# Four turns per head in the first mixer's recurrence, with the next head's decays spread over them

## The chip, the core and the metric

One core of one Trainium2 chip. The metric is the device time of one execution in microseconds; lower is better. The engines are TensorE (PE), VectorE (DVE), ScalarE (ACT), GpSimd (POOL) and SyncE (SP), which here issues the loads.

## What is computed

Two transformer blocks in a row on 256 tokens of width 1024. The first has a mixer (a gated linear recurrence in both directions and a latent attention, merged by gates), a mixture of 64 experts and a gated side input; the second a convolution and window attention. The change lies in the first mixer, whose core is, cut to what matters:

```
z = rmsnorm(x, ln_mix) @ w_in
q_a, f_fw, f_bw, i_a, og_a, c_q, c_kv, k_rope, gate_a, gate_b = split(z)
# recurrence, 4 heads of 128, each direction, chunks of 64
g = cumsum(log_f)
decay = exp(where(lower, g[t] - g[s], -inf))
scores = einsum('tk,sk,tsk->ts', q, k, decay)        # k = 1 - f
o = (q * exp(g)) @ state + scores @ v
o_hg = rmsnorm(o_fw + o_bw, hg_onorm) * silu(og_a)
y_a = o_hg @ w_oA
# latent attention, 8 heads of 96
qm = rope(rmsnorm(rmsnorm(c_q) @ w_uq));  km = rope(rmsnorm([rmsnorm(c_kv) @ w_ukv, k_rope]))
y_b = attention(qm, km, vm) @ w_oB
x = x + (sigmoid(gate_a) * y_a + sigmoid(gate_b) * y_b) @ w_out
```

## The kernel before

All matmuls of the big projections are exact to float32 by splitting: `split` (L185) casts a weight slice of 128x512 to `hi` on ACT (L188) and computes the rest `lo` on DVE or, by the pattern in `sub_turn`, on POOL (L192); "v" means all on DVE, "vg" turn about. `gemm_t` (L235, matmuls L247 to L249) and `gemm_nat` (L197, L209 to L211) take eight such slices for one 512-wide chunk and yield after each two. I call two slices, 24 matmuls in `gemm_t`, a step. Weights come in tiles of 1 MB through a ring of buffers (`wload`, L108); a tile's load is issued when the buffer's last reader is done.

The order on PE is that of the program text (`manual_schedule`, L347). `weave` (L263) runs generators turn about, so the yields decide how matmuls of several parts are mixed. On the other engines a planner orders the instructions by its own estimate of when each is ready, and may run one ahead of its place in the text; `tc.issue_after(ins)` puts the instructions of a block behind `ins` on that engine, and only on that.

The stages around the change, in order:

1. `first_lane` (two decay chunks of `w_in`, 8 steps, then logarithms L589 and scans L594) woven with `latent_prepare` (L432): norms of the latent vectors, projection of keys, then of queries, and `head_norm` (L403) for each half of the tokens. `head_norm` squares on ACT, sums and scales on DVE, makes four rotary products on POOL (L425 to L428) and combines them on DVE (L429, L430).
2. `modulation(16, 8)` (matmuls L655), then two steps of `second_lane` (the q chunk), then the rest of `second_lane` (q, v, og) woven with `latent_attend` (L496), which also takes the pieces of head 0's decays. In `second_lane` the two halves of k are added (L633), multiplied by q, and summed by 128x1 matmuls with `ones` (L640) into a PSUM bank.
3. `recurrence` (L764) woven with `modulation(0, 16)` and `gate_lane` (four gate chunks and `w_oB`, 20 steps): in each round one turn of the recurrence, one modulation step while there are any, one gate step.

`decayed(h)` (L679) makes a head's factors: R and L for seven levels by subtraction (R on DVE L692, L on POOL L694), exponentials on ACT (L698, L700, L704 to L716), R times q on DVE (L717), L times k per level (L721, levels 0, 2, 4 on POOL, the others on DVE), and the cross factors CR and CL (L724, L726). In `recurrence` a head has three turns: the diagonal, the cross scores (L802) and levels 0 to 3 (L812), each level copied into `sct` under a mask by DVE (L815); levels 4 to 6; then `attend` for the head before (L768), `finish` for the one before that (L787), and all of the next head's decays at once.

PSUM has four banks "mm", three "ps", one "ob".

Of the kernel before, what the change touches and what calls it, by code (L numbers as in the profile page):

```python
# [20 lines left out]
P = 128  # L21
# [58 lines left out]
def kernel(ctx: ExitStack, tc: tile.TileContext, a: dict, out: bass.AP, dbg=None):  # L80
# [182 lines left out]
    def weave(*lanes):  # L263
        live = list(lanes)
        stop = object()
        while live:
            for lane in list(live):
                g, n = lane
                for _ in range(n):
                    if next(g, stop) is stop:  # L270
                        live.remove(lane)
                        break

    def both(done):
        def each(ps):
            for i in range(NT):
                done(i, ps[i])
        return each
# [124 lines left out]
    def head_norm(dst, which, i):  # L403
# [23 lines left out]
        G.tensor_tensor(t[:, 2], x2, cb, op=ALU.mult)  # L427
        G.tensor_tensor(t[:, 3], x1, sb, op=ALU.mult)  # L428
        V.tensor_tensor(x1, t[:, 0], t[:, 1], op=ALU.subtract)  # L429
        V.tensor_tensor(x2, t[:, 2], t[:, 3], op=ALU.add)  # L430

    def latent_prepare():  # L432
# [26 lines left out]
        V.tensor_copy(kgain[:, 64:96], rrow("k_norm")[:, 64:96])  # L459
        yield  # L460
        khl = [split(sp, wuk, c * 512, 512) for c in range(2)]
        for i in range(NT):
# [10 lines left out]
            V.tensor_copy(kn[:, i * MH:(i + 1) * MH, 64:96], misc[:, i, 384:416][:, None, :].to_broadcast([P, MH, 32]))  # L473
            head_norm(kn, 1, i)
        yield
        for c in range(2):
            qhl = [split(sp, wuq, k * 768 + c * 384, 384) for k in range(2)]
            for i in range(NT):
                o = bank("ps")
                for k in range(2):  # L480
# [6 lines left out]
                               o[:, :384].rearrange("p (h d) -> p h d", h=4))  # L487
        for i in range(NT):
            head_norm(qn, 0, i)
        dump("qm", qn)  # L490
# [100 lines left out]
    def scan_decays(d):  # L591
# [5 lines left out]
        if d:  # L597
            V.tensor_scalar(ge[:, 1, :, 0:4], last, -1.0, None, op0=ALU.mult)
            V.tensor_add(ge[:, :, :, 4], ge[:, :, :, 0], ge[:, :, :, 1])
            V.memset(gxv[:, :, :, 0:1], 0.0)  # L600
        else:
            V.tensor_copy(ge[:, 0, :, 0:4], last)

# [19 lines left out]
    def first_lane():  # L623
        yield from gemm_t(sp, hT, chunk("w_in", 0), take_decay(0))
        yield from gemm_t(sp, hT, chunk("w_in", 1), take_decay(1))
        log_decays()
        for d in range(2):
            scan_decays(d)

    def second_lane():  # L630
        yield from gemm_t(sp, hT, chunk("w_in", 2), take_q)
        qk = qg[:, 1]
        V.tensor_tensor(qk, kT[:, 0], kT[:, 1], op=ALU.add)  # L633
        V.tensor_tensor(qk, qk, qT, op=ALU.mult)
        yield from gemm_nat(sp, hT, chunk("w_in", 3), 512, take_v)
        b = bank("ps")
        for h in range(HGH):
# [41 lines left out]
    def decayed(h):  # L679
# [38 lines left out]
        for l in range(NLEV):  # L718
            eng = V if l % 2 or l == 6 else G
            Ls = both_sides(L[:, l], l)  # L720
            eng.tensor_tensor(Ls, Ls, sides(kT, (X, HGH * 256 + X + (1 << l)), 1, l), op=ALU.mult)  # L721
            if l in (0, 3):
                yield
# [3 lines left out]
        yield R, L, CR, CL  # L727

    def decayed_at_once(h):
        return list(decayed(h))[-1]  # L730

# [8 lines left out]
    cc = cc_cm.__enter__()  # L740
    sub_turn[1] = "vg"
    weave((modulation(16, 8), 1))
    second = second_lane()
    weave((some(second, 2), 1))
    weave((latent_attend(), 1), (second, 1))

# [17 lines left out]
    def recurrence():  # L764
# [29 lines left out]
        for h in range(HGH):  # L794
# [9 lines left out]
            nc.scalar.copy(cr, dg[:, :256])  # L804
            scores[h] = (sct, cr)
            for l0 in range(0, NLEV, 2):
                n = min(2, NLEV - l0)
# [6 lines left out]
                for l in range(n):  # L814
                    V.copy_predicated(sct, msk[:, l0 + l][:, None, :].to_broadcast([P, NT, P]),  # L815
                                      b[:, l * 256:(l + 1) * 256].rearrange("p (i t) -> p i t", i=NT))
                if l0 in (2, 6):
                    yield
            if h >= 1:
                attend(h - 1)  # L820
            if h >= 2:
                finish(h - 2)
            if h + 1 < HGH:
                RL[h + 1] = decayed_at_once(h + 1)
            yield
# [1047 lines left out]
```

## Time and profile before

| | us |
|---|---|
| median of 3 runs (lowest, highest) | 1122.52 (1121.57, 1122.76) |
| the profiled execution, own time | 1120.88 |
| its span, first to last instruction | 1119.1 |
| PE busy in the span | 1026.4 (92%) |
| DVE busy | 570.7 (51%) |
| ACT busy | 423.3 (38%) |
| POOL busy | 294.9 (26%) |
| stages: first mixer to about 262 us, experts to about 745 us, then side input and second block | |

Times are microseconds from the start of the span. An engine's busy time covers pipelined matmuls, whose ends are modelled: a matmul of 0.28 us can start 0.12 us after the one before. The granted clock is a share of TensorE's 2.4 GHz. In a timeline a row joins like instructions in sequence; brackets give the idle time of the engine before it and what ended that.

### The profile page before, as it was taken

What the parts mean: (1) busy time and instruction counts of PE and PEld (TensorE: products, weight loads), DVE (VectorE), ACT (ScalarE), POOL (GpSimd) and SP (SyncE); (2) the same over time, 40 slices, a digit from 0 to 9 for tenths busy, and PEclk for the clock granted to TensorE, in tenths of its full rate; (3) what the DMA queues carried; (4) which work ended last, traced back from release to release, by engine and by line L of the source; (5) the groups of instructions that cost most, each with busy time, mean ns of one, the idle gap of its engine ahead of it and who ended that gap; (6) DMA issues with size and microseconds to landing.
All of it is one profiled execution on the core that took longest, in us unless ns stands there. A gap on an engine that the chain in (4) does not pass through costs nothing.

```text
span 1119.1 us, 17631 instructions
## 1 busy us (share of the span) xinstructions
PE 1026.4 (92%) x6844; PEld 730.9 (65%) x6848; DVE 570.7 (51%) x1157; ACT 423.3 (38%) x875; POOL 294.9 (26%) x255
## 2 busy tenths in 40 slices
PE   8999989998999768999987788799999999999997
PEld 6887679985444224444333233267889989999996
DVE  6977996364333212221122232285847798852465
ACT  6767854440101031010110020263457546545553
POOL 1554474440000000000000000003543363554462
PEclk9999999999999889999997899998999999999999
DMA  9673566878999999999999999963554343345531
GB/s 351 236 264 114 220 233 263 339 293 330 421 421 419 421 420 421 420 422 420 421 420 419 421 421 418 421 268 99 171 201 167 136 139 131 128 160 184 184 114 39
DMA packets 47259, 321.49 MB, mean 287 GB/s; under 512 B 5761, under 2 KB 6273, under 8 KB 9410
## 3 DMA queue, kind: packets, MB, share of 16 engines
q1 hardware_dynamic: 47090, 320.04, 72.5%
q8 instruction: 56, 0.92, 0.4%
q14 instruction: 33, 0.27, 0.1%
q0 software_dynamic: 80, 0.26, 0.1%
HBM read 319.23 MB, written 1.05 MB: 286 GB/s over the span
## 4 chain that ended last, share of the span: by engine, by line
PE 58%; DMA 23%; DVE 12%; ACT 3%; issue 3%; POOL 1%; SPq 0%; DVEq 0%; POOLq 0%; ACTq 0%
DMA w<-in_w_dram 21%; PE mm L249 8%; PE mm L247 8%; PE mm L248 8%; PE mm L1257 5%; PE mm L209 3%; PE mm L210 3%; PE mm L211 3%; PE ps L1224 3%; PE mm L1297 3%; PE ps L1240 2%; PE mm L971 2%; DVE lo L192 2%; PE ps L174 2%; DMA w<-in_w_ple_proj_dram 2%
## 5 line engine op out<-in xcount | busy, mean ns | idle before, releaser
L188 ACT CAST hi<-w 128x512 fp32r<-128x512 f32 (+2 forms) x340 | 205.3, 616 | 177.8 <-PE mm L248 127.4
L192 POOL TENSOR_TENSOR lo<-w,hi 128x512 fp32r<-128x512 f32 x144 | 200.4, 1394 | 237.9 <-ACT hi L188 231.5
L192 DVE TENSOR_TENSOR lo<-w,hi 128x512 fp32r<-128x512 f32 (+2 forms) x196 | 148.4, 767 | 113.5 <-ACT hi L188 103.7
L1257 PE MATMUL mm<-w,xe 128*32 128x512 f32 x1024 | 128.7, 641 | 29.3 <-DMA w<-in_w_dram 21.9
L247 PE MATMUL mm<-h,hi 128*128 128x256 f32 x448 | 129.5, 289 | 0.0
L249 PE MATMUL mm<-h,lo 128*128 128x256 f32 x448 | 126.7, 283 | 0.1
L248 PE MATMUL mm<-h,hi 128*128 128x256 f32 x448 | 126.6, 283 | 0.0
L1257 PEld LDWEIGHTS mm<-w,xe 128*32 128x32 f32 x1024 | 30.5, 114 | 114.9 <-issue 61.7
L1279 DVE SCALAR_TENSOR_TENSOR th<-th,mm 128x256 f32<-128x256 f32 x16 | 6.7, 421 | 179.6 <-ACT th L1278 179.6
L247 PEld LDWEIGHTS mm<-h,hi 128*128 128x128 f32 x448 | 85.6, 191 | 3.1 <-issue 3.1
L249 PEld LDWEIGHTS mm<-h,lo 128*128 128x128 f32 x448 | 85.6, 191 | 0.3 <-DVE lo L192 0.3
L248 PEld LDWEIGHTS mm<-h,hi 128*128 128x128 f32 x448 | 85.7, 191 | 0.0
L1278 ACT ACTIVATE th<-mm 128x256 f32<-128x256 f32 x16 | 6.1, 383 | 191.0 <-PE mm L1257 174.4
L1297 PE MATMUL mm<-w,hE 128*32 128x512 f32 x512 | 61.8, 608 | 15.5 <-DMA w<-in_w_dram 10.8
L1242 DVE TENSOR_TENSOR acc<-acc,ps 128x512 f32<-128x512 f32 x60 | 41.2, 687 | 62.6 <-PE ps L1240 62.6
L1224 PEld LDWEIGHTS ps<-G,x 128*128 128x128 f32 x512 | 62.0, 201 | 16.1 <-issue 14.4
L1352 POOL DMA_DIRECT2D tabs<-in_tabs_dram x1 | 0.7, 737 | 270.3 <-DMA w<-in_w_dram 270.3
L249 PE MATMUL mm<-hT,lo 128*128 128x256 f32 x224 | 65.2, 291 | 6.4 <-DVE lo L192 6.4
L1240 PE MATMUL ps<-y,cT 128*128 128x512 f32 x128 | 61.7, 625 | 9.8 <-ACT y L1303 9.8
L247 PE MATMUL mm<-hT,hi 128*128 128x256 f32 x224 | 66.4, 297 | 0.0
L1224 PE MATMUL ps<-G,x 128*128 128x128 f32 x512 | 65.2, 288 | 0.5 <-DVE G L1216 0.5
L169 POOL TENSOR_TENSOR s<-s,half 128x1 f32<-128x1 f32 (+1 forms) x6 | 4.0, 668 | 233.4 <-DVE s L167 233.4
(475 smaller groups left out, 2131.5 us busy)
## 6 DMA issues: line engine op xcount, KB each, us to landing
w<-in_w_dram SPq DMA_DIRECT2D x192, 1024.0 KB, 19.8
w<-in_w_in_dram SPq DMA_DIRECT2D x66, 1024.0 KB, 4.9
w<-in_w_mod_dram SPq DMA_DIRECT2D x12, 1024.0 KB, 9.3
w<-in_w_out_dram SPq DMA_DIRECT2D x4, 1024.0 KB, 6.6
w<-in_w_ple_gate_dram SPq DMA_DIRECT2D x4, 1024.0 KB, 13.7
w<-in_w_out_conv_dram SPq DMA_DIRECT2D x4, 1024.0 KB, 4.7
w<-in_w_out_attn_dram SPq DMA_DIRECT2D x4, 1024.0 KB, 4.8
w<-in_w_o_dram SPq DMA_DIRECT2D x4, 1024.0 KB, 4.8
```

The costliest lines, as they stand in the source:

```text
L188: nc.scalar.copy(hi[:, :n], wt[:, off:off + n])
L192: last_sub[eng is G] = eng.tensor_sub(lo[:, :n], wt[:, off:off + n], hi[:, :n])
L209: mm(ps[m][:, :n], ah, wh, start=kt == 0, stop=False)
L210: mm(ps[m][:, :n], al, wh, start=False, stop=False)
L247: mm(o, hi[:, c:c + P], ah, start=kt == 0 and b % 2 == 0, stop=False)
L248: mm(o, hi[:, c:c + P], al, start=False, stop=False)
L249: mm(o, lo[:, c:c + P], ah, start=False, stop=kt == kts - 1 and b % 2 == 1)
L1224: mm(b[:, k * P:(k + 1) * P], x[:, i, kt * P:(kt + 1) * P], Gt[i].rearrange("p e s -> p (e s)"), start=i == 0, stop=i == 1)
L1240: mm(b, cT[:, i * P:(i + 1) * P], y[:, c * 512:(c + 1) * 512], start=True, stop=True)
L1242: V.tensor_add(acc[:, i, s_], (acc if q else x)[:, i, s_], b)
L1257: mm(ps[32 * j:32 * j + 32, :], xe[:, kt, 32 * j:32 * j + 32], wt[:, j * 512:(j + 1) * 512], start=kt == 0, stop=kt == KT - 1)
L1297: mm(ps[32 * j:32 * j + 32, :], hE[:, ft, 32 * j:32 * j + 32], wt[:, j * 512:(j + 1) * 512], start=ft == 0, stop=ft == 1)
```

## The change

`head_norm` yields between the rotary products and their sums. For keys it is run up to that yield; after the query projection `latent_prepare` yields four times, and then the key sums and the whole query norm follow, their DVE instructions behind the last DVE split made so far. `scan_decays` returns its last instruction, and the key-half sum is issued behind it. The pattern "vg" begins two steps later, so that four more splits stay with DVE alone by pattern. The `ones` matmuls use a bank of "mm". All seven products of L are DVE's. A head of the recurrence has four turns, the last head three: the next head's decays start in the first turn (levels 0 to 2 of the subtractions), go on in the second (the other subtractions and the two big exponentials), in the third (the small exponentials, R times q, L of levels 0 and 1) and end in the fourth; the DVE instructions of the first two pieces stand behind the last copy into `sct` made in that turn.

```diff
+    def then(*made):
+        order = ExitStack()
+        for m in made:
+            order.enter_context(tc.issue_after(m.ins))
+        return order
...
         G.tensor_tensor(t[:, 3], x1, sb, op=ALU.mult)
+        yield
         V.tensor_tensor(x1, t[:, 0], t[:, 1], op=ALU.subtract)
...
+        turns = []
...
-            head_norm(kn, 1, i)
+            turns.append(head_norm(kn, 1, i))
+            next(turns[i])
         yield
...
-        for i in range(NT):
-            head_norm(qn, 0, i)
+        for _ in range(4):
+            yield
+        with then(last_sub[False]):
+            for g in turns:
+                weave((g, 1))
+            for i in range(NT):
+                weave((head_norm(qn, 0, i), 1))
...
-            V.memset(gxv[:, :, :, 0:1], 0.0)
-        else:
-            V.tensor_copy(ge[:, 0, :, 0:4], last)
+            return V.memset(gxv[:, :, :, 0:1], 0.0)
+        return V.tensor_copy(ge[:, 0, :, 0:4], last)
...
-            scan_decays(d)
+            scanned[0] = scan_decays(d)
+
+    scanned = [None]
...
-        V.tensor_tensor(qk, kT[:, 0], kT[:, 1], op=ALU.add)
+        with then(scanned[0]):
+            V.tensor_tensor(qk, kT[:, 0], kT[:, 1], op=ALU.add)
...
-        b = bank("ps")
+        b = bank("mm")
...
         for l in range(NLEV):
-            eng = V if l % 2 or l == 6 else G
             Ls = both_sides(L[:, l], l)
-            eng.tensor_tensor(Ls, Ls, sides(kT, (X, HGH * 256 + X + (1 << l)), 1, l), op=ALU.mult)
-            if l in (0, 3):
+            V.tensor_tensor(Ls, Ls, sides(kT, (X, HGH * 256 + X + (1 << l)), 1, l), op=ALU.mult)
+            if l in (1, 4):
                 yield
...
-    sub_turn[1] = "vg"
     weave((modulation(16, 8), 1))
     second = second_lane()
     weave((some(second, 2), 1))
+    sub_turn[1] = "vg"
     weave((latent_attend(), 1), (second, 1))
...
+            ahead = decayed(h + 1) if h + 1 < HGH else None
             for l0 in range(0, NLEV, 2):
...
                 for l in range(n):
-                    V.copy_predicated(sct, msk[:, l0 + l][:, None, :].to_broadcast([P, NT, P]),
-                                      b[:, l * 256:(l + 1) * 256].rearrange("p (i t) -> p i t", i=NT))
+                    copied = V.copy_predicated(sct, msk[:, l0 + l][:, None, :].to_broadcast([P, NT, P]),
+                                               b[:, l * 256:(l + 1) * 256].rearrange("p (i t) -> p i t", i=NT))
                 if l0 in (2, 6):
+                    if ahead:
+                        with then(copied):
+                            weave((some(ahead, 1 if l0 == 2 else 3), 1))
                     yield
...
-            if h + 1 < HGH:
-                RL[h + 1] = decayed_at_once(h + 1)
+            if ahead:
+                next(ahead)
+                yield
+                RL[h + 1] = list(ahead)[-1]
             yield
```

## Rows read from the trace of the kernel before

**Rows 1.** Windows of all engines: busy us (x instructions), granted clock, DMA share, GB/s

```profile
50.00:60.00 10.00, 7.56 (x56) 7.21 (x58) 10.00 (x20) 4.02 (x7) 8.96 (x12) 0.83 0.51 188
127.00:190.00 63.00, 56.51 (x464) 49.88 (x461) 55.97 (x96) 33.08 (x81) 37.92 (x37) 1.00 0.75 287
190.00:262.00 72.00, 71.70 (x499) 64.89 (x499) 38.06 (x72) 33.68 (x67) 28.85 (x23) 1.00 0.78 300
300.00:400.00 100.00, 85.34 (x612) 36.51 (x610) 27.73 (x64) 10.12 (x24) 0.00 (x0) 0.93 1.01 420
```

**Rows 2.** Waits of SyncE's DMA queue, 28 to 262 us: us, times, longest

```profile
SPq L110 <- DVE lo L192: 110.0, 22, 12.8
```

**Rows 3.** Waits of PE, 28 to 190 us: us in total, times, longest

```profile
PE mm L249 <- DVE lo L192: 6.4, 4, 2.5
PE ps L812 <- DVE sct L815: 5.1, 3, 2.0
PE ps L640 <- ACT qk L504: 1.5, 1, 1.5
PE ob L529 <- ACT pT L538: 0.5, 1, 0.5
```

**Rows 4.** Timeline of DVE: start us, us, line, operation, [idle before <- releaser]

```profile
49.73 0.53 DVE L429 TENSOR_TENSOR kn<-rt 128x128 f32<-128x128 f32 x1 [0.78 <-POOL rt L428]
...
51.84 2.40 DVE L192 TENSOR_TENSOR lo<-w,hi 128x512 fp32r<-128x512 f32 x3
```

**Rows 5.** Timeline of DVE ahead of the second stall

```profile
67.15 1.18 DVE L633 TENSOR_TENSOR qg<-kT 128x1024 f32<-128x1024 f32 x1
...
69.64 2.29 DVE L594 TENSOR_TENSOR_SCAN gx<-ek,lfT 128x1024 f32<-128x1024 bf16 x1
71.84 0.67 DVE L192 TENSOR_TENSOR lo<-w,hi 128x512 fp32r<-128x512 f32 x1
```

**Rows 6.** Timeline of PE: the three waits for `lo`, and matmuls behind the first

```profile
52.57 0.58 PE L249 MATMUL mm<-hT,lo 128*128 128x256 f32 x1 [2.44 <-DVE lo L192]
52.95 0.41 PE L247 MATMUL mm<-hT,hi 128*128 128x256 f32 x1
...
55.93 0.28 PE L249 MATMUL mm<-hT,lo 128*128 128x256 f32 x1
56.04 0.28 PE L247 MATMUL mm<-hT,hi 128*128 128x256 f32 x1
...
72.56 0.39 PE L249 MATMUL mm<-hT,lo 128*128 128x256 f32 x1 [2.55 <-DVE lo L192]
...
141.65 0.38 PE L249 MATMUL mm<-hT,lo 128*128 128x256 f32 x1 [1.26 <-DVE lo L192]
```

**Rows 7.** Timeline of ACT: the last logarithms, and the copy behind C

```profile
65.36 1.69 ACT L589 ACTIVATE lfT<-lfT,lbw 128x256 f32<-128x256 f32 x4
...
103.10 0.60 ACT L504 COPY qk<-ps 128x512 f32<-128x512 f32 x1
```

**Rows 8.** Groups of DVE, 126.9 to 190 us: busy us, mean ns, idle before

```profile
L692 DVE TENSOR_TENSOR R<-gx 128x256 f32<-128x256 f32 x18 | 11.2, 684 | 0.0
L192 DVE TENSOR_TENSOR lo<-w,hi 128x512 fp32r<-128x512 f32 x11 | 8.8, 802 | 1.8 <-ACT hi L188 1.8
L721 DVE TENSOR_TENSOR L<-L,kT 128x256 f32<-128x256 f32 x12 | 8.6, 752 | 0.0
L717 DVE TENSOR_TENSOR R<-R,qg 128x1792 f32<-128x1792 f32 x3 | 6.1, 2024 | 0.3 <-ACT R L698 0.3
```

**Rows 9.** Timeline of DVE: R for head 0, L with POOL silent, R for head 2

```profile
97.05 1.09 DVE L692 TENSOR_TENSOR R<-gx 128x256 f32<-128x256 f32 x3
...
131.27 0.41 DVE L721 TENSOR_TENSOR L<-L,kT 128x256 f32<-128x256 f32 x1
...
141.51 4.12 DVE L692 TENSOR_TENSOR R<-gx 128x256 f32<-128x256 f32 x6
```

**Rows 10.** Groups of POOL, 126.9 to 190 us

```profile
L721 POOL TENSOR_TENSOR L<-L,kT 128x256 f32<-128x256 f32 x9 | 8.2, 941 | 5.9 <-ACT L L700 5.9
```

More of the change, by code (lines that the diff above doesn't have):

```diff
@@ L727, in decayed @@
         yield R, L, CR, CL
-    def decayed_at_once(h):
-        return list(decayed(h))[-1]
     weave((first_lane(), 1), (latent_prepare(), 1))
```

## The prediction

> **What bounds the kernel now.** I read the windows first, to see where TensorE (PE) is short of work. From 190 us on, the first mixer keeps PE busy for 71.7 of 72 us; in the 63 us before, it is busy for 56.5, with VectorE (DVE) at 56.0 [rows 1]. Behind the mixer the expert weights stream at 420 GB/s [rows 1], and every load of the mixer waits for a buffer that a `lo` or a matmul frees, DVE's `lo` alone ending 110 us of such waits [rows 2]. So the stream has no start of its own: it starts when the mixer lets go, and I take what the mixer gains or loses one to one into the end of the program.
>
> Then I read who made PE wait between 28 and 190 us [rows 3]. Four waits for a DVE `lo` make 6.4 us (2.44, 2.55, 1.26 [rows 6] and a rest of about 0.2), three for the copies into `sct` make 5.1, one for ScalarE's (ACT) `qk` copy 1.5, one for `pT` 0.5. Only these can be won.
>
> Last, what DVE did ahead of each wait. At 49 us it had finished a key gain, stood 0.78 us behind a rotary sum whose POOL products were not there, then did `lo` late [rows 4]. At 70 us the next `lo` stood behind the key-half sum and the second scan [rows 5]. In the recurrence six subtractions for the next head, 4.12 us [rows 9], went ahead of a copy of the present head for which PE then waited.
>
> **The change, part by part.**
>
> *A. Rotary sums and query norms behind the last split.* PE's order is not touched: the yields hold no matmul. The `lo` that came at 51.84 us can follow the gain directly, at 49.0, before PE asks (about 50.1). Won: the wait of 2.44 us, and the half-rate matmuls behind it. From 52.95 to 55.93 us 14 matmuls start 0.21 us apart, and at 0.12 us from there on [rows 6]: after PE had stood idle the granted clock was at 1.2 GHz instead of 2.4, 0.83 on the mean from 50 to 60 us [rows 1], and 2.98 - 14 x 0.12 = 1.3 us went that way. A = 3.74 us. Bounds 0 (the wait moves to the next step) and 3.74; I take the upper, as nothing else stands ahead of that `lo`. What is late instead: the sums and the query norms. Their cover is the modulation's matmuls and two gemm steps, which stand between this gemm and the first transposes of queries; if that is gone, it is the rival of B.
>
> *B. The second stall.* Worth 2.55 + 1.3 (half-rate matmuls again, taken as in A) = 3.85 us. The key-half sum, 1.18 us [rows 5], goes behind the scans; its reader is a product 15 us later, so I price it at nothing, and at 1.2 us if a `lo` queues behind it. The second scan still needs the last logarithm, which ended at 65.36 + 1.69 = 67.05 us [rows 7]. All of this comes 3.7 us earlier: 63.3, plus 2.29 for the scan and 0.67 for the `lo`, is 66.3; PE, too, asks 3.7 us earlier than at 70.0, that is at 66.3. Even, so one DVE instruction in between shows: I leave 0.6 us. B = 3.25; bounds 0 (but see the rival) and 3.85. The first four splits of this gemm are all DVE's now: two more at about 0.7 us, in the cover of the modulation; POOL loses as many, which eases its queue.
>
> *C. The dot-product bank.* The matmuls with `ones` took a bank that ACT had to empty by `qk`, which it came to at 103.10 us [rows 7]: a wait of 1.5 us [rows 3]. The other set of banks is free of it. But attention passes from ACT to DVE to PE and back, and ACT is as late for the next step. I take half, 0.75; bounds 0 and 1.5. The og gemm's banks move on by one, to one that the `v` scaling empties in time; nothing for that, 0.5 us if ACT is late.
>
> *D. The recurrence.* Waits to win: 5.1 + 1.26 = 6.4 us. It is an account of DVE's work against PE's cover. Cover: a fourth gate step stands ahead of the scores of heads 1, 2 and 3, 24 matmuls at 0.12 us, 2.9 each, 8.6 us in all (these steps came later before, so they cost PE nothing). Work added to DVE: one more `lo` per head (the other is POOL's), 3 x 0.80 = 2.4 us; and three products of L per head that POOL did, nine. One costs 0.41 us where POOL is silent [rows 9] and 0.75 on the mean of this stretch [rows 8]: 3.7 to 6.8, middle 5.2. Work that falls away: DVE is slow where POOL works beside it. R takes 0.36 us in the attention before and 0.68 on the mean here, L 0.41 and 0.75 [rows 8, 9]: 18 x 0.32 + 12 x 0.34 = 9.8 us of such excess. Of POOL's 37.9 us [rows 1] 8.2 are the products of L [rows 10], 22%: 2.2 us of the excess go with them. Net on DVE 2.4 + 5.2 - 2.2 = 5.4 against 8.6 of cover: the shortage falls by 3.2 us. D = 3.2. Bounds: 6.4 (the copies now go ahead of the next head's work, so order alone could end every wait) and -0.6 (dear products, no relief).
>
> The finish of head 3 comes three rounds later, in the 19th of 20 gate steps; the gemm that reads it follows the 20th, so one step of 2.9 us covers it. No load is added; those of `w_in` and `w_mod` follow their buffers as before.
>
> Sum: 3.74 + 3.25 + 0.75 + 3.2 = 10.9 us, 1%. The profiled execution took 1120.88 us (span 1119.1), so 1110.0 for it; it lay 1.64 us under the median of the runs, which gives 1122.52 - 10.9 = **1111.6 us**.
>
> **The rivals.**
>
> *The stall moves (14%).* Norms, sums and scans are one lump behind the last split. If the scans start no earlier than before, the `lo` of 71.84 us stays there while PE asks at 66.3. It waits 5.5 us where it waited 2.55, so B turns to -2.95 and 3.74 - 2.95 + 0.75 + 3.2 = 4.7 remain: 1117.8. For it: DVE is busy for long stretches there. Against: the scans wait for logarithms, and these follow PE.
>
> *DVE is the scarce engine (9%).* Nine products move onto an engine that is busy for 56 of 63 us. At 0.75 us and with no relief from POOL the account is 8.6 - 2.4 - 6.8 = -0.6: the recurrence gains nothing, and 1122.5 - 7.7 + 0.6 = 1115.4 is left. Against: the 0.41 us product. The Trainium skill (Perfetto Trace Analysis, "Optimizing Scalar/DVE Operations") says that with VectorE saturated work may go to ScalarE or even to GpSimd, so this change goes the wrong way; by it 1115.4. The same section warns that the two share a read port, so that such a move might not help; the rows of single and mean durations are on that side.
>
> *A longer chain in the recurrence, slower (8%).* The next head's subtractions may no longer run ahead: they wait for the copies, in two pieces. If DVE in fact gets to them only after the second turn, all R subtractions (6 x 0.68), the R product (2.02), seven L (5.3) and two `lo` (1.6) [rows 8] stand in a row, 13.0 us, against two gate steps, 5.8 us: 7.2 us of waiting per head, 21.6 for three where 6.4 were, so 1122.5 - 7.7 + 15.2 = 1130.0. It decides from 5.5 us of waiting per head: then A, B and C are eaten and 2.2 us on top. Against: the first three subtractions have a turn of their own, and the order after the second copy leaves two more.
>
> *Nothing arrives (5%).* The stream sets the end whenever the mixer ends: 1122.5. Against: the loads' waits for buffers [rows 2].
>
> **How the numbers follow.** The forecast has 64%. A difference of 0.2%, about 2.2 us, is what a measurement of this kernel can tell from none. Faster by more: forecast, moved stall and scarce DVE, 0.87; within it, nothing arrives, 0.05; slower, the long chain, 0.08. The range: with every term at its upper bound and the 0.5 us of the `pT` wait, 3.74 + 3.85 + 1.5 + 6.4 + 0.5 = 16.0, so 1106.5; upward it takes in both cases of smaller gain, to 1118.0. Outside lie 13% of cases and some of the tails.
>
> **What the profile would show.** A right: no wait of PE for `lo` near 46 to 56 us, and a granted clock of 1.00 there. B right: the wait of 2.55 us near 66 us is under 1 us; wrong: it is over 3. C: the `ones` matmuls wait for nothing, with a smaller wait at the next transposes. D right: `sct` waits under 3 us in sum and the nine products at about 0.5 us; wrong: PE waits for L or R of the next head at its first score matmuls. The whole is wrong if the stretch from 28 to 262 us shortens and the first weight-bound expert does not come earlier by as much.

## The result, and the profile after

| | before | changed |
|---|---|---|
| median (lowest, highest), us | 1122.64 (1121.57, 1123.70) | 1109.59 (1108.27, 1112.36) |
| profiled execution, its span | 1120.88, 1119.1 | 1110.49, 1108.7 |
| ratio, 95% interval | | 0.9885 (0.9867 to 0.9903) |

The kernel is faster by 13 us, 1.15%; 1111.6 was forecast, with a range of 1106.5 to 1118.0. The sum was nearly met, but not by its terms: the first stall went as forecast, the second grew, and about a third of the gain lies outside the mixer.

First the windows of the changed kernel (columns as in [rows 1]):

```profile
50.00:60.00 10.00, 10.00 (x118) 8.25 (x117) 10.00 (x25) 7.80 (x15) 8.08 (x12) 1.00 0.76 247
62.00:72.00 10.00, 6.01 (x38) 5.80 (x37) 8.72 (x17) 3.41 (x7) 6.43 (x6) 0.73 0.82 342
127.00:190.00 63.00, 60.48 (x491) 55.44 (x490) 54.91 (x100) 33.82 (x71) 34.75 (x27) 0.97 0.79 302
300.00:400.00 100.00, 82.52 (x561) 34.45 (x560) 25.37 (x59) 13.78 (x30) 0.70 (x1) 0.89 1.01 420
```

From 50 to 60 us PE has all it can do at a granted clock of 1.00; it had 7.56 us at 0.83. From 62 to 72 us it has only 6.01, at 0.73. In the window from 127 to 190 us it is busy for 60.5 of 63 us where it was for 56.5; the recurrence begins at 127.0 us in before and at 122.4 here, and the granted clock fell to 0.97, so these two are not quite alike. The weight stream behind runs at 420 GB/s as before. The waits of PE from 28 to 222 us (us in total, times, longest), beside [rows 3]:

```profile
PE mm L249 <- DVE lo L192: 6.7, 3, 4.0
PE ps L174 <- ACT pr L530: 0.9, 2, 0.7
PE ob L543 <- DVE obT L546: 0.4, 1, 0.4
```

The copies into `sct` and the `qk` copy are gone from the list. The `lo` waits are not: three of them make 6.7 us where four made 6.4. The timeline of PE has the two long ones:

```profile
68.36 0.58 PE L249 MATMUL mm<-hT,lo 128*128 128x256 f32 x1 [3.99 <-DVE lo L192]
...
160.76 0.39 PE L249 MATMUL mm<-hT,lo 128*128 128x256 f32 x1 [2.52 <-DVE lo L192]
```

The waits of the load queue for a DVE `lo`, 110.0 us in [rows 2], are 105.3 from 28 to 255 us:

```profile
SPq L110 <- DVE lo L192: 105.3, 22, 11.2
```

The next table takes the first matmul of each stage from the timeline of PE and gives the time from one to the next, in us. "Again" are the profiles of the same kernels in the runs below; "pinned" is the last experiment, which has the mixer of before.

| from, to | before | again | pinned | changed | again |
|---|---|---|---|---|---|
| start, decay chunks | 24.29 | 24.84 | 22.50 | 22.78 | 22.62 |
| decay chunks, modulation (term A) | 35.44 | 35.40 | 33.98 | 31.29 | 31.32 |
| modulation, first query transposes | 9.45 | 9.45 | 9.45 | 9.45 | 9.45 |
| to the first attention scores (B) | 8.05 | 8.06 | 8.99 | 10.26 | 10.55 |
| to the first cross scores (C) | 49.79 | 52.09 | 54.61 | 48.65 | 49.95 |
| to the output projection (D) | 102.64 | 102.65 | 102.66 | 99.31 | 96.67 |
| to the first expert matmul | 39.33 | 39.32 | 39.33 | 39.33 | 39.35 |
| experts and gate, to the first matmul of h with hi | 560.55 | 561.65 | 560.09 | 558.07 | 558.92 |
| to the end | 289.59 | 289.58 | 289.59 | 289.57 | 289.59 |

From the decay chunks to the output projection that is 199.0 and 197.9 us against 205.4 and 207.7 before: the mixer gave 6.4 us in one pair of profiles and 9.7 in the other. The start gave 1.5 to 2.2 us, in which nothing was changed: the pinned kernel shows 22.50 there without the change, and over all profiles of this document it takes 22.4 to 24.8, so that part is chance. The stretch behind the first expert matmul gave 2.5 and 2.7 us, and no line of it was edited. The last experiment comes back to it.

The granted clock of a stage is part of these differences. In C's stage it was 1.00, 0.97 and 0.94 in the three profiles of the mixer of before, which took 49.8, 52.1 and 54.6 us there, with waits that differ by 1.4 us at most. In D's stage of the changed kernel it was 0.98 in the first profile (99.31 us) and 1.00 in the second (96.67). So stages are compared below at like clocks where the rows allow it.

**Term A.** No `lo` wait stands between 28 and 62 us, and the clock is 1.00.

**Term B.** Here is what DVE did ahead of the wait of 3.99 us:

```profile
59.93 2.55 DVE L608 TENSOR_TENSOR_SCAN gx<-ek,lfT 128x1024 f32<-128x1024 bf16 x1
...
63.94 1.23 DVE L423 TENSOR_SCALAR rqs<-rq 128x8 f32<-128x8 f32 x1 [0.66 <-POOL rq L169]
65.09 0.16 DVE L424 TENSOR_SCALAR rqs<-rq 128x8 f32<-128x8 f32 x1
...
65.44 2.29 DVE L608 TENSOR_TENSOR_SCAN gx<-ek,lfT 128x1024 f32<-128x1024 bf16 x1
67.64 0.67 DVE L192 TENSOR_TENSOR lo<-w,hi 128x512 fp32r<-128x512 f32 x1
...
68.54 1.20 DVE L649 TENSOR_TENSOR qg<-kT 128x1024 f32<-128x1024 f32 x1
```

and POOL beside it:

```profile
60.30 3.61 POOL L169 TENSOR_TENSOR rq<-rq,half 128x8 f32<-128x8 f32 x1
63.88 1.27 POOL L192 TENSOR_TENSOR lo<-w,hi 128x512 fp32r<-128x512 f32 x1
```

The key-half sum (L649) did go behind the scans and behind the `lo`. But the query norms, which term A had moved here, end in two scalings of 128x8 elements (L423, L424). They wait for a power that POOL makes (L169); it took 3.61 us beside the first scan, against 1.93 for its twin 4 us earlier. The scalings and the second scan stand ahead of the `lo`, which PE asked for at 64.4 (68.36 less 3.99) and got at 68.3. Counted from the first matmul of the decay chunks, PE asked 4.1 us earlier than in before, and the second scan began only 2.7 us earlier [rows 5].

**Term D.** The second long wait, at 160.76, has another cause. ACT first:

```profile
155.49 1.49 ACT L714 ACTIVATE R<-R 128x1536 f32<-128x1536 f32 x1 [3.80 <-DVE R L708]
156.88 1.12 ACT L188 CAST hi<-w 128x512 fp32r<-128x512 f32 x2
```

then DVE:

```profile
157.01 2.03 DVE L733 TENSOR_TENSOR R<-R,qg 128x1792 f32<-128x1792 f32 x1
158.95 1.75 DVE L192 TENSOR_TENSOR lo<-w,hi 128x512 fp32r<-128x512 f32 x1
```

ACT stood 3.80 us with nothing to do, because the exponential of R at the head of its queue waited for DVE's subtractions; the two `hi` casts behind it could have run, since the last L248 matmuls on the slices before ended at 152.7 and 154.1 us, which is what such a cast waits for elsewhere in this trace. On DVE the `lo` of these then stood behind R times q, until 159.0. The Trainium skill (PSUM — Partial Sum Buffer, "Engine vs sequencer instructions") calls the queues of ScalarE, VectorE and GpSimd strict FIFOs; these rows agree.

The groups of DVE from 122 to 222 us (busy us, mean ns, idle before), beside [rows 8]:

```profile
L192 DVE TENSOR_TENSOR lo<-w,hi 128x512 fp32r<-128x512 f32 x25 | 20.3, 818 | 11.0 <-ACT hi L188 11.0
L736 DVE TENSOR_TENSOR L<-L,kT 128x256 f32<-128x256 f32 x21 | 12.6, 658 | 0.0
L708 DVE TENSOR_TENSOR R<-gx 128x256 f32<-128x256 f32 x18 | 9.0, 551 | 0.0
```

Products and subtractions of all three later heads lie in both windows. The nine products more cost 12.6 - 8.6 = 4.0 us, and R got cheaper by 11.2 - 9.0 = 2.2.

### The profile page after: what moved, and what is told of

It reads as the page before. It is cut to its first block, busy times and chain, and to the rows that moved or that the text cites. A ratio compares the mean times of both kernels' runs of the same rounds, so it can differ in the third digit from the quotient of the medians.

```text
span 1108.7 us, 17634 instructions
## 1 busy us (share of the span) xinstructions
PE 1026.3 (93%) x6844; PEld 728.9 (66%) x6848; DVE 572.8 (52%) x1171; ACT 423.2 (38%) x875; POOL 287.9 (26%) x241
## 4 chain that ended last, share of the span: by engine, by line
PE 63%; DMA 20%; DVE 11%; ACT 3%; issue 2%; POOL 1%; SPq 0%; DVEq 0%; POOLq 0%; ACTq 0%
DMA w<-in_w_dram 18%; PE mm L247 8%; PE mm L249 8%; PE mm L248 8%; PE mm L1275 5%; PE mm L209 3%; PE mm L211 3%; PE mm L210 3%; PE ps L1242 3%; PE mm L1315 3%; PE ps L1258 3%; PE mm L1149 2%; DVE lo L192 2%; PE ps L174 2%; PE mm L989 2%
## 5 line engine op out<-in xcount | busy, mean ns | idle before, releaser
L192 DVE TENSOR_TENSOR lo<-w,hi 128x512 fp32r<-128x512 f32 (+2 forms) x198 | 151.4, 776 | 103.0 <-ACT hi L188 93.6
L1275 PE MATMUL mm<-w,xe 128*32 128x512 f32 x1024 | 132.1, 655 | 27.8 <-DMA w<-in_w_dram 20.6
L248 PE MATMUL mm<-h,hi 128*128 128x256 f32 x448 | 126.6, 283 | 0.0
L1275 PEld LDWEIGHTS mm<-w,xe 128*32 128x32 f32 x1024 | 30.8, 115 | 115.5 <-issue 60.5
L248 PEld LDWEIGHTS mm<-h,hi 128*128 128x128 f32 x448 | 85.7, 191 | 0.0
L169 POOL TENSOR_TENSOR s<-s,half 128x1 f32<-128x1 f32 (+1 forms) x6 | 3.6, 605 | 235.3 <-DVE s L167 235.3
```

Source lines behind the costliest of these rows:

```text
L192: last_sub[eng is G] = eng.tensor_sub(lo[:, :n], wt[:, off:off + n], hi[:, :n])
L248: mm(o, hi[:, c:c + P], al, start=False, stop=False)
L1275: mm(ps[32 * j:32 * j + 32, :], xe[:, kt, 32 * j:32 * j + 32], wt[:, j * 512:(j + 1) * 512], start=kt == 0, stop=kt == KT - 1)
```

## The experiments

Ratios are to the kernel before, run beside them; those of the changed kernel are 0.9885 (above) and 0.9902 (below).

**The changed kernel again.** No edit.

> The changed kernel once more. In the one profile pair seen so far, 6.4 us of the span's 10.4 were won between 24 and 238 us of the mixer; 1.5 us came before 24 us, where no edit lies, and 2.5 us after the mixer, around 750 us, where matmuls ran at half rate in the kernel before and not after. Theory: these 4 us are the clock's and chance, so they may be there or not in this profile, with the mixer's part the same within 0.3 us: the router's first transposes 215.3 us after the projection of 416 columns has ended. Rival: they belong to the change, then start and end repeat: the 416-column projection over by 22.8 us and no half-rate matmuls at 750 us. Median 1108 to 1112 either way.

Measured: 1111.97 us, ratio 0.9902 (0.9886 to 0.9919). The wait near 64 us came again (4.0 us), the one near 160 was 1.4 us, and no low clock followed it: 96.67 us instead of 99.31. The start was short again, and the mixer was 1.1 us shorter, where I had expected it alike within 0.3. Two profiles of one kernel differ by 2.6 us in this stage, and by up to 4.8 in C's (the three of the mixer of before), so I trust no stage to less unless its clock is compared as well. Done so, D's stage is narrow: of the versions with its four turns unchanged, four profiles have a `lo` wait of 1.4 us near 160, a clock of 1.00 and 96.7 us, and four have a wait of 2.1 to 2.5, a clock of 0.98 and 98.8 to 99.3 us.

**The kernel before again.** No edit, one run.

> The kernel before, a second profile. Theory (the half-rate matmuls at 15 us and at 755 us in its first profile are chance): the projection of 416 columns ends at 22.5 to 22.9 us and no 3 us are lost at 750 us, with the mixer from there to the router's transposes 221.7 us within 1 us. Rival (they belong to this program): 24.3 us and 3 us again.

Measured: 1124.73 us, span 1123.1. The start was 24.84 us, against 22.5 to 22.9 expected, so the 1.5 us there looked like part of the change until `before_pin` showed 22.50 with the same instructions up to there.

**Norms early.** Rotary sums and query norms back where they were; the rest of the change stays.

```diff
-        yield
...
-            turns.append(head_norm(kn, 1, i))
-            next(turns[i])
+            head_norm(kn, 1, i)
...
-        for _ in range(4):
-            yield
-        with then(last_sub[False]):
...
+        for i in range(NT):
+            head_norm(qn, 0, i)
```

> Head norms whole and where they were before, all else as changed. Theory (the late norms win 4.2 us at the first stall and lose 2.1 at the second, since their last scaling stands ahead of the second scan): the wait of 2.4 us with its half-rate matmuls is back near 48 us, the wait of 4.0 us near 64 becomes 0 to 2.5 us, and the mixer ends 1.5 to 2.5 us later than in the changed kernel, about 1111.5. Rival (the stall only moves, so the place of the norms is worth nothing): within 0.5 us of the changed kernel.

Measured: 1112.00 us, ratio 0.9901 (0.9885 to 0.9918), so the same time as with them late. The first stall is back (A's stage 33.98 us), but B's takes 5.25 us instead of 10.26, and the mixer is the shorter one: 33.98 + 9.45 + 5.25 + 48.78 + 96.67 = 194.1 us against 197.9 and 199.0. My expectation had it longer. (norms_pin below, with the same mixer, took 197.5 us in all with 5.05 in B's stage; but with a clock of 0.83 behind the first stall and 0.98 in D's stage; so B's row is firm, the sum is not.) Its waits from 28 to 225 us:

```profile
PE mm L249 <- DVE lo L192: 5.2, 4, 2.4
PE mm L249 <- POOL lo L192: 1.1, 1, 1.1
```

With the norms early the edits of term B (the later key-half sum and the later "vg", not told apart here) are worth 8.05 - 5.25 = 2.8 us, close to the 3.25 forecast; with them late, A's 4.1 us costs B more than it gains. The terms are right one at a time and don't add. What the sum gained was lost again behind the router, 562.3 us instead of 558.1 and 558.9; see the last experiment.

**L on POOL.** Levels 0, 2 and 4 of the products of L go back to POOL.

```diff
-            V.tensor_tensor(Ls, Ls, ...
+            eng = V if l % 2 or l == 6 else G
+            eng.tensor_tensor(Ls, Ls, ...
```

> The products of L of levels 0, 2 and 4 on GpSimd again, all else as changed. Theory (VectorE's two-input instructions stretch while GpSimd works beside them, so the nine products cost less on VectorE than their neighbours lose): recurrence 1 to 3 us longer, from the first cross score to the end of the gates 100.3 to 102.3 us where the changed kernel took 99.3. Rival (VectorE is the scarce engine): 1 to 3 us shorter, 96.3 to 98.3. If neither is over 0.5 us, the place of these products does not matter now.

Measured: 1113.09 us, ratio 0.9902 (0.9883 to 0.9920); D's stage 101.12 us, 1.8 and 4.5 more than in the two profiles with all of them on DVE, the 1.8 at the same clock of 0.98; the `lo` waits rose from 6.7 to 7.8. The program's time does not tell the two apart. The rule that the prediction quoted from the Trainium skill (Perfetto Trace Analysis, "Optimizing Scalar/DVE Operations": offload a saturated VectorE) gains nothing here; its warning on the shared port is the half that fits.

**Three turns.** All of the next head's decays at once, as before, the rest of the change kept.

```diff
-            ahead = decayed(h + 1) if h + 1 < HGH else None
...
-                    if ahead:
-                        with then(copied):
-                            weave((some(ahead, 1 if l0 == 2 else 3), 1))
                     yield
...
-            if ahead:
-                next(ahead)
-                yield
-                RL[h + 1] = list(ahead)[-1]
+            if h + 1 < HGH:
+                RL[h + 1] = list(decayed(h + 1))[-1]
```

> Three turns per head and the next head's decays in one piece without a place behind the copies, as before; products of L on VectorE. Theory (cover of a fourth gate step, 2.9 us per head, against VectorE's work): waits of 4 to 6 us come back at the copies or at the next head's first scores, 1113 to 1116. Rival (silent GpSimd alone took the waits away): waits under 2 us, within 1 us of the changed kernel.

Measured: 1113.10 us, ratio 0.9915 (0.9898 to 0.9933); D's stage 102.12 us. Before had 102.65: without the fourth turn 0.5 us of D's gain is left in this profile; the program's time does not tell it from the changed kernel's. The waits for copies stayed away even so; what came is a `lo` wait of 4.46 us at 140.27, behind six products of L in one row on DVE:

```profile
133.25 6.04 DVE L736 TENSOR_TENSOR L<-L,kT 128x256 f32<-128x256 f32 x6
139.20 0.43 DVE L827 COPY_PREDICATED sct<-msk,ps 128x256 f32<-128x256 uint8 x1
139.53 0.68 DVE L192 TENSOR_TENSOR lo<-w,hi 128x512 fp32r<-128x512 f32 x1
```

**The bank of before.** The `ones` matmuls use a "ps" bank again; one run.

> Changed kernel with the matmuls by ones in a bank of ps again. Theory of the sum (the wait of 1.5 us is half won): from the first scores to the first cross score 49.4 us where the changed kernel took 48.6 to 49.9 and the kernel before 49.8. Rival (the wait is won in full): 50.1. Rival (it only moves to the next transposes): 48.7.

Measured: 1115.32 us, span 1113.7. The wait for `qk` is back with 1.8 us, and C's stage takes 52.05 us, above all three values that I had named; that is 2.1 us more than in the second profile of the changed kernel, at about the same clock (0.97, there 0.96). The recurrence gives nothing of it back: 96.73 us at a clock of 1.00, where the second profile has 96.67 at 1.00. The mixer took 31.28 + 9.45 + 9.25 + 52.05 + 96.73 = 198.8 us, 0.9 more than there, since B's stage, which lies ahead of this edit, happened to be 1.3 us shorter. The rest of the time of this run comes from its start (24.43) and from the experts' stage (561.5). It is one profile.

**The scalings behind the second scan.** L423 and L424 for both halves are issued behind the scans.

```diff
+            late.append((hs, r_))
-            V.tensor_scalar(rqs[:, 0, hs], r_, -scale, ...
-            V.tensor_scalar(rqs[:, 1, hs], r_, scale, ...
...
+    with then(scanned[0]):
+        for hs, r_ in late:
+            V.tensor_scalar(rqs[:, 0, hs], r_, -scale, ...
+            V.tensor_scalar(rqs[:, 1, hs], r_, scale, ...
```

> Changed kernel, but the two scalings of the query norm that make rqs are issued behind the second scan (on VectorE) instead of ahead of it. Theory: these scalings wait for GpSimd's power (63.9 us) and hold the second scan from about 63.2 to 65.4 us, and the lo that PE asks for at 64.3 stands behind the scan. Then the scan runs 63.2 to 65.4, lo ends near 66.0, the wait of 4.0 us becomes 1 to 2 us without half-rate matmuls behind it, and the stretch from the first query transposes to the first scores takes 6 to 7 us instead of 10.3 to 10.6. Rival (the scan is late because the logarithms or the first scan are): the stretch stays over 9 us.

Measured: 1107.67 us, ratio 0.9865 (0.9842 to 0.9889). B's stage 8.39 us (10.26 and 10.55; 6 to 7 expected), the wait 3.1 us instead of 4.0.

**The second scan behind a low half.** The scan of the second direction is issued behind the `lo` of the third step of the q chunk.

```diff
-        for d in range(2):
-            scanned[0] = scan_decays(d)
+        scan_decays(0)
...
-        yield from gemm_t(sp, hT, chunk("w_in", 2), take_q)
+        for n, _ in enumerate(gemm_t(sp, hT, chunk("w_in", 2), take_q)):
+            if n == 2:
+                with then(last_sub[False]):
+                    scanned[0] = scan_decays(1)
+            yield
```

> Changed kernel, but the second scan is issued behind the lo of the third step of the q gemm. Theory (it is only the order on VectorE, the scan has no early reader): lo comes as soon as its hi, near 63.3 us, PE does not wait, and the stretch from the first query transposes to the first scores takes 4.2 to 5.2 us instead of 10.3 to 10.6. Rival (the wait moves one step on: the scan starts GpSimd's six subtractions, 5.3 us, ahead of the next lo): a wait of 2 to 4 us in the step after, and less than half of the gain at the first cross score.

Measured: 1108.27 us, ratio 0.9877 (0.9846 to 0.9908). B's stage 7.35 us (4.2 to 5.2 expected), but with two waits where there was one, as the rival had it; by the first cross scores only 0.3 and 1.9 us of the gain are left against the two profiles of the changed kernel:

```profile
PE mm L249 <- DVE lo L192: 3.4, 3, 1.8
PE mm L249 <- POOL lo L192: 1.9, 1, 1.9
```

Each of the two takes part of the stall away, so the instructions named above do make it. The waits that are left suggested that both together end it.

**Both behind the low half.** The two edits in one, with the scalings also behind the third step's `lo`.

> The changed kernel with the two short scalings and the second scan both behind the low half that TensorE waits for. Theory (what stands ahead of that low half on VectorE is the stall): the wait of 4.0 us near 64 us falls below 1.5, no half-rate stretch follows it, the stretch from the first query transposes to the first scores takes 5.2 to 6.2 us (10.3 to 10.6 in the changed kernel, 8.4 and 7.4 with one part each), and the time is 1104.5 to 1107 (ratio 0.983 to 0.986). Rival (VectorE has too much work by then, and the wait only moves to the next low halves): the stretch takes 7 us or more, or a new wait of over 1.5 us stands near 72 us, and the time is 1107 to 1108.5, as with one part each.

Measured: 1109.01 us, ratio 0.9873 (0.9853 to 0.9893): the rival's side. B's stage shrank to 3.94 us, less than the theory had, and C's grew to 53.84 from 48.65 and 49.95. The waits:

```profile
PE mm L249 <- POOL lo L192: 4.6, 1, 4.6
PE mm L249 <- DVE lo L192: 2.2, 2, 2.1
```

The stall went on to the next low half that POOL makes, since there six subtractions of L stood ahead of it, which need the second scan:

```profile
70.07 4.87 POOL L717 TENSOR_TENSOR L<-gx 128x256 f32<-128x256 f32 x6 [3.46 <-DVE gx L615]
74.91 2.58 POOL L192 TENSOR_TENSOR lo<-w,hi 128x512 fp32r<-128x512 f32 x2
```

**And the subtractions in one turn.** As the last, and all of the next head's subtractions in the first turn, so that ACT's exponential finds its operands ready.

```diff
-                            weave((some(ahead, 1 if l0 == 2 else 3), 1))
+                            weave((some(ahead, 2), 1))
```

> As rqs_scan, and the six subtractions of the next head's decays all in one turn, so that the exponential on ScalarE doesn't stand ahead of the hi casts and wait for them. Theory (the low-half wait near 157 us is a queue order on ScalarE): that wait, 1.4 to 2.5 us in every run of the change so far, falls below 0.6, the stretch from the first cross score to the output projection takes 95 to 96.3 us (96.7 at best so far), and the time is 0.5 to 1.5 us below rqs_scan. Rival (VectorE is short of time in the recurrence, and any order moves the wait): another low-half or copy wait of over 1 us appears between 122 and 215 us, the stretch takes 96.5 us or more, and the time is that of rqs_scan or above.

Measured: 1110.41 us, ratio 0.9883 (0.9865 to 0.9901): the rival again. DVE's `lo` waits fell to 0.2 us where rqs_scan had 2.2, so the queue order on ACT did make the wait near 160; but the six subtractions now meet on POOL too, and D's stage is 99.11 us (98.79 in rqs_scan):

```profile
PE mm L249 <- POOL lo L192: 8.3, 3, 4.6
PE mm L249 <- DVE lo L192: 0.2, 1, 0.2
```

```profile
131.01 8.19 POOL L717 TENSOR_TENSOR L<-gx 128x256 f32<-128x256 f32 x6 [5.14 <-PE ps L832]
139.15 2.53 POOL L192 TENSOR_TENSOR lo<-w,hi 128x512 fp32r<-128x512 f32 x2
```

None of these versions is shown to beat the changed kernel: the lowest, 0.9865 (0.9842 to 0.9889), overlaps with 0.9885 and 0.9902.

**The order behind the experts.** By then the profiles fell into two groups from the first expert matmul to the first matmul of h with hi: 560.6 to 562.3 us for before (twice), the old bank and the early norms, 556.4 to 558.9 for the rest. In that stretch the planner had written another order in the two groups. `x3g` in the expectations is the product on DVE that the second block's first transposes read. The last two kernels put, by order edges, the additions, low halves and gate tanhs of that stretch into the order of the changed kernel.

```diff
-    with tc.issue_after(taken.ins):
+    with tc.issue_after(taken.ins), tc.issue_after(added[0].ins):
         weave((some(lane, 1), 1))
...
-    weave((some(lane, 1), 1))
+    with tc.issue_after(added[1].ins):
+        weave((some(lane, 1), 1))
...
-    weave((some(lane, 3), 1))
+    weave((some(lane, 2), 1))
+    with tc.issue_after(gated[0, 1][0].ins), tc.issue_after(gated[0, 1][1].ins):
+        weave((some(lane, 1), 1))
```

> The kernel before, its mixer untouched; only the stretch behind the last experts is put into the order that the changed kernel has there (additions and low halves in turn on VectorE, two gate tanhs ahead of the last two hi casts on ScalarE), by four order edges. Theory (a part of the change's gain is this order, which the planner chose anew 480 us after the edit): from the first expert matmul to the first matmul of h with hi the ten profiles so far fall into two groups, 560.6 to 562.3 us in the four with the old order and 556.5 to 558.9 in the six with the new one; this run falls into the second, its wait for x3g is 0.9 us instead of 2.2, no half-rate stretch follows it, and the time is 3 to 4 us below before (ratio 0.9965 to 0.9975). Rival (the order is incidental, the difference comes from when the experts start or by chance): the stretch takes 560.6 to 562.3 us and the time is that of before within 1 us.

Measured: 1122.66 us, ratio 0.9990 (0.9975 to 1.0005); the stretch 560.1 us, the wait for x3g 1.5, and a new one of 0.9 for a `hi`.

> The changed kernel with the norms undone, as in norms_early, and the order behind the last experts put as in the changed kernel. Theory (norms_early had the shorter mixer, 210.5 against 214.3 to 215.3 us to the router, and lost it again only because its order behind the experts fell back to the old one): the mixer stays at 210 to 211 us, the stretch from the first expert matmul to the first matmul of h with hi falls from 562.3 to 556.5 to 558.9, and the time falls from 1112.0 to 1107 to 1109 (ratio 0.986 to 0.988). Rival (the time behind the router is set by something that waits for no mixer, a stream or a limit of its own): the time stays at 1111 to 1113.

Measured: 1112.07 us, ratio 0.9914 (0.9886 to 0.9943); the stretch 559.7 us, the wait for x3g 2.3.

Both missed their times. Divided at the matmuls of `gtp` with ones, which follow those of the gate, the stretch says more than its sum. Times are from one first matmul to the next in us; `pT` is the gate's input.

| | experts, to the first of `pT` | to `gtp` with ones | to h with hi | wait for x3g | clock in the 20 us behind `gtp` |
|---|---|---|---|---|---|
| before | 456.35 | 24.50 | 79.70 | 2.2 | 0.83 |
| before_again | 457.54 | 24.49 | 79.62 | 2.2 | 0.83 |
| norms_early | 459.31 | 24.49 | 78.50 | 2.2 | 0.91 |
| ps_bank | 458.58 | 24.47 | 78.49 | 2.3 | 0.91 |
| norms_pin | 456.23 | 25.10 | 78.38 | 2.3 | 0.91 |
| before_pin | 457.90 | 25.98 | 76.21 | 1.5 | 1.00 |
| the eight other profiles | 456.3 to 458.8 | 24.5 | 75.6 to 75.7 | 0.9 | 1.00 |

The experts' own part varies by 3 us whatever the kernel. Behind `gtp` the two groups are sharp: the wait for x3g and the low clock that follows it are worth 2.8 to 4.1 us. So before_pin did win 3.4 to 3.5 us there; it lost 1.5 ahead of `gtp`, where its edges made the new wait for a `hi`, and its experts' part was 0.4 and 1.5 us longer than in before. In norms_pin the edges won nothing.

The rows show what they left as it was. DVE's idle time for `hi` casts in that stretch, in the changed kernel:

```profile
728.72 6.12 DVE L192 TENSOR_TENSOR lo<-w,hi 128x512 fp32r<-128x512 f32 x10 [1.68 <-ACT hi L188]
```

in norms_early:

```profile
724.63 0.69 DVE L192 TENSOR_TENSOR lo<-w,hi 128x512 fp32r<-128x512 f32 x1 [1.62 <-ACT hi L188]
...
727.24 5.51 DVE L192 TENSOR_TENSOR lo<-w,hi 128x512 fp32r<-128x512 f32 x9 [1.91 <-ACT hi L188]
```

and still in norms_pin and in before_pin:

```profile
726.74 0.69 DVE L192 TENSOR_TENSOR lo<-w,hi 128x512 fp32r<-128x512 f32 x1 [1.68 <-ACT hi L188]
...
729.34 5.50 DVE L192 TENSOR_TENSOR lo<-w,hi 128x512 fp32r<-128x512 f32 x9 [1.91 <-ACT hi L188]
```

```profile
741.15 6.11 DVE L192 TENSOR_TENSOR lo<-w,hi 128x512 fp32r<-128x512 f32 x10 [3.76 <-ACT hi L188]
```

In all of these ACT casts twelve `hi` in a row, and the edges did not reach their order within the row. In the changed kernel the last two slices of the gate's first half stand seventh and eighth. In the three kernels of the longer stretch (four profiles) the last of them stands twelfth, in norms_pin too, and in before_pin both stand at the end; the rows above fit that, since DVE's idle time ends as the seventh, the twelfth or the eleventh cast does. DVE takes them in the order of the text, and idles 1.9 to 2.1 us more. All seven kernels with the twelve in the changed kernel's order took 556.4 to 558.9 us (eight profiles), all five others 559.7 to 562.3 (six). So the place of these casts goes with the time without exception, but it was not changed alone: that it is the whole cause is argued, not shown. What is shown is where the time goes, the wait for x3g and the clock behind it, and that the orders I pinned do not bring back the 75.6 us.

## Why the prediction was right, and where it was wrong

**The total** came out 2 us from the forecast because errors cancelled: B is off by about 5.5 us, and 4 to 5 us came from where nothing was forecast.

**A, right.** 3.74 was forecast; the stage fell by 4.1 us against before and 2.7 against before_pin, which had the same wait without the slow clock, as norms_early had. The 1.4 us between is the clock's share, forecast as 1.3. The wait is gone and the clock is 1.00, as said.

**B, wrong.** 3.25 was forecast, and the stage grew by 2.2 to 2.5 us: close to the -2.95 of the rival that the stall moves. The wait is 4.0 us, over the 3 that were named as wrong. The step that failed is "Even, so one DVE instruction in between shows: I leave 0.6 us". I had timed the second scan by its logarithm alone, and put the query norms of A into the cover of the modulation. They were not covered: their power on POOL, slowed to 3.61 us beside the scan, and the scalings behind it came between the two scans. "All of this comes 3.7 us earlier" is where it shows: PE asked 4.1 us earlier, the second scan began 2.7 us earlier. So the rival's own reason, scans no earlier than before, did not hold either; the stall grew for a third. norms_early shows the 2.8 us of B where A is not made, rqs_behind_scan and scan_behind_lo that it is these instructions which eat them. Another part needs no norms: in before_pin, where only the low clock at the first stall was absent, PE came 1.4 us earlier to the second one, waited 3.65 us there instead of 2.55, and B's stage took 8.99 instead of 8.05. So a part of what is won at the first stall is lost at the second even with the instructions of before.

**C, at least as large as forecast, by single profiles.** 0.75 forecast. At a clock of 1.00 the stage fell from 49.79 to 48.65 us, at 0.97 and 0.96 from 52.09 to 49.95; undoing the bank adds 2.1 at a like clock. So half of the wait, as I took it, looks too little, though other edits bear on this stage too.

**D, right in direction, too small in size.** 3.2 was forecast, 3.3 and 6.0 came. The 6.0 is the pair at a clock of 1.00 (102.64 and 96.67), near my upper bound of 6.4, and 96.7 came in four profiles; the 3.3 has the low clock behind the new `lo` wait in it, so that its nearness to 3.2 is luck. The waits for copies are gone, as said; a `lo` wait of 1.4 to 2.5 us behind ACT's exponential has taken their place, which I had nowhere. DVE's account: the products cost 4.0 us more, 0.44 each (5.2 in mine), R 2.2 less, which is the relief I had reckoned with; with these two the account gives 8.6 - 2.4 - 4.0 + 2.2 = 4.4. Undoing the fourth turn leaves 0.5 us of the gain, undoing the move of L 1.5, at clocks of 0.97 and 0.98.

**One to one to the end, only in part.** From the output projection to the first expert matmul and in the last 289.6 us nothing moved, as assumed. But 2.5 to 2.7 us were won in the stretch behind the first expert matmul (4.0 and 4.1 behind `gtp`, less what the experts lost by chance), and norms_early lost there 3.4 and 4.2 us of a mixer that was 3.8 and 4.8 us shorter. A change in the mixer is also a new draw of the planner's order, about 500 us behind the last stage that was edited.

**What stays open.** Whether the mixer as a whole is bound by the work on DVE and POOL ahead of the `lo`: all the versions but three_turns and l_on_pool took 194.1 to 199.0 us from the decay chunks to the output projection, with quite different stalls, and the edges that ended one wait began another. No run took work away from both engines.

## What to carry to other kernels

When late work is moved off one stall, list what already stands at the place where it lands, on every engine that feeds it, and price both moves together; two gains at neighbouring stalls don't add if the same low half waits for both. Where a planner writes the order, compare the instruction orders of the whole program, far from the edit too, before a stage's gain is put down to the edit. Compare a stage at like granted clocks: two profiles of one kernel can differ by more than the edit is worth.

## What the runs showed of the hardware

The same wait does not always bring the low clock. PE waited 2.44 us for the first late `lo` in before [rows 6], in before_again and in before_pin, with the same instructions up to there. From 50 to 60 us the granted clock was 0.83 on the mean in before [rows 1] and in before_again; in before_pin the wait ended at 50.77, and the same window has

```profile
50.00:60.00 10.00, 9.23 (x110) 7.55 (x110) 10.00 (x21) 6.62 (x11) 9.72 (x11) 1.00 0.45 146
```

with 1.00. The two kernels with the norms early, which have the same wait of 2.44 us, show both as well: 1.00 in norms_early, 0.83 in norms_pin. A's stage takes 34.0 us with the one and 35.4 with the other.

DVE instructions with two operands in SBUF took longer beside POOL. In before_pin the key-half sum took 2.30 us where [rows 5] have 1.18, and a short product behind it 0.16:

```profile
65.00 2.30 DVE L633 TENSOR_TENSOR qg<-kT 128x1024 f32<-128x1024 f32 x1
67.22 0.16 DVE L660 TENSOR_TENSOR modT<-th,vec 128x16 f32<-128x16 f32 x1
```

```profile
64.92 1.30 POOL L192 TENSOR_TENSOR lo<-w,hi 128x512 fp32r<-128x512 f32 x1 [2.72 <-ACT hi L188]
```

In before POOL's `lo` came after the sum had begun, and the short product paid:

```profile
68.25 1.26 DVE L660 TENSOR_TENSOR modT<-th,vec 128x16 f32<-128x16 f32 x1
```

```profile
68.16 1.32 POOL L192 TENSOR_TENSOR lo<-w,hi 128x512 fp32r<-128x512 f32 x1 [3.81 <-ACT hi L188]
```

The excess of 1.12 and 1.10 us is nearly the 1.30 of POOL's `lo`. From the first scan to the second DVE took 5.3 us in both, so the longer wait behind it in before_pin is not this but the earlier PE. The Trainium skill (SBUF — State Buffer, "Who interferes with whom") says that such a DVE instruction contends with a GpSimd instruction that reads SBUF; the rows agree. Which of the two pays is not fixed. In the changed kernel six products of L run at 0.36 us each from 129.41, and at 0.91 each from 139.82:

```profile
129.41 2.16 DVE L736 TENSOR_TENSOR L<-L,kT 128x256 f32<-128x256 f32 x6
...
139.82 5.46 DVE L736 TENSOR_TENSOR L<-L,kT 128x256 f32<-128x256 f32 x6
```

and POOL was at work beside both:

```profile
129.66 3.66 POOL L192 TENSOR_TENSOR lo<-w,hi 128x512 fp32r<-128x512 f32 x1 [4.52 <-ACT hi L188]
...
137.98 4.58 POOL L192 TENSOR_TENSOR lo<-w,hi 128x512 fp32r<-128x512 f32 x2
```

The first time DVE had begun, and POOL's one `lo` took 3.66 us, against 1.27 in the row of 63.88 above; the second time POOL had begun, and DVE's products took two and a half times as long, while POOL's two `lo` took 2.3 us each, so that both paid. What decides who pays was not tested. So the price of a product, on which the account of term D rests, hangs on the moment at which it runs.
